# Second feed-forward matmul of a hybrid encoder block: groups 0 and 1 of the first pass interleaved, and a row load moved behind the pass

## The chip, the cores and the metric

The kernel runs on one core of one Trainium2 chip. The metric is the device time of one execution in microseconds (us), as the median of several runs. TensorE (PE) does the matmuls, VectorE (DVE) and ScalarE (ACT) prepare operands and evacuate results, GpSimd (POOL) does very little, and SyncE (SP) issues every DMA that loads weights, on one queue and in program order.

## The reference

One layer of an encoder block on 512 positions with 1024 channels, all in float32. What matters here is its end, the feed-forward part and the final norm:

```
xn = modulate(rmsnorm(h, norm2_g[l]), sh2, sc2)
ff = jnp.square(jax.nn.relu(xn @ w_ff1[l])) @ w_ff2[l]
h = h + g2[:, None, :] * ff
...
return rmsnorm(h, final_g)
```

`w_ff1` is 1024 x 4096 and `w_ff2` is 4096 x 1024. Before it come the two branches of the block (a gated MLP and a matrix-memory recurrence), which the change does not touch.

## The kernel before, in words

**Precision.** Every float32 matmul is made of three matmuls (`mm3`, L116 to L119): each operand is split into a high part (a copy rounded to the matmul's type, made on ScalarE) and a low part (the rest, a subtraction on VectorE), and the products high-high, low-high and high-low are added in PSUM. So for each operand there is one ACT instruction and one DVE instruction, and then TensorE can go on.

**The second feed-forward matmul.** The first 3072 of the 4096 rows of `w_ff2` are taken in six groups of 512 rows, `GROUPS = "WWSWWS"` (L1032). A "W" group is multiplied by Winograd's form of Strassen's scheme, with 7 products of half blocks in place of 8; an "S" group is multiplied plainly. The work is done in two passes over the six groups, because the PSUM banks hold only some of the sums at a time. In the first pass a W group has four products, P1, P2, P7 and P3, and in the second pass three (`later`, L1037). One product of one group is a **step**: two row halves of 128 positions times two k-tiles times three matmuls, so 12 matmuls of 128 x 512. The list `plan_` (L1131) says which sum each step adds to, and the loop at L1196 walks it; step 0 is its first entry. The banks of P1, P2, P7 and P3 (`gP1..`, `gP2..` and so on) are shared by all groups of the pass.

**The operands of a step.** The generator `passes` (L1096) yields them in the plan's order: a left operand out of the activations (`hl`, L1084: `hsh` on ACT at L1092 and `hsl` on DVE at L1093, 128 x 512) and a weight operand (`w_pair`, L1068: `wh` on ACT at L1075 and `wl` on DVE at L1076, 128 x 1024). The loop keeps five operand pairs made ahead (`prefetch_step(5)`). The names are numbered by step: `wh_g0`, `wh_g1`, `wh_g2`, `wh_x3`, `wh_x4`, `wh_g5` are steps 0 to 5; three of every five steps use the slots that the earlier matmul used too (`_g`, three buffers) and two use slots of their own (`_x`, two buffers, in a memory pool that opens with this stage).

**Where the weights come from.** For a W group the block of `w_ff2` has a left half (columns 0 to 511) in two pieces, `F11` and `F21`, and a right half in two pieces, `F12` and `F22`. Each piece is one DMA of 512 KB. P1 uses F11 and P2 uses F21 just as loaded. P7 needs the difference F22 - F12 (a DVE subtraction, L1106 in this version), and P3 uses F22. Left pieces are loaded into three buffers that the first feed-forward matmul also uses, so the first three are issued while that matmul still runs, and every split of a left piece frees its buffer for the next (`left.more()`). Right pieces go into a pool of four buffers that takes the place of the memory that held the first matmul's operands; it opens only when that matmul has read them (`x2s.close()`, `mhs.close()`, L1143 and L1144), and then four right pieces are asked for (L1150, L1151).

**The final norm's row.** `fing`, the vector `final_g` repeated over the 128 partitions (512 KB), is asked for at L1147, between the closing of the old pools and the first right pieces. Only the very last part of the kernel reads it (L1268).

**What sets the order.** The kernel is written in program order, and a scheduler then places each engine's instructions; each engine runs its own list strictly in that order. On SP the list is the order in which DMAs are issued: an entry that waits holds all entries behind it.

After the passes the last 1024 rows of `w_ff2` follow plainly (L1242), and then the gated residual and the final norm (L1253 on).

Of the kernel before, what the change touches and what calls it, by code (L numbers as in the profile page):

```python
# [16 lines left out]
P = 128  # L17
# [32 lines left out]
def block_kernel(ctx, tc, vecs_d, rows_d, ws_d, x_d, w_ada, w_in, w_out, w_ff1, w_ff2, out_d):  # L50
    nc = tc.nc
    act, dve, pool, pe, sp = nc.scalar, nc.vector, nc.gpsimd, nc.tensor, nc.sync
# [554 lines left out]
    n = 0  # L607
# [302 lines left out]
    hq = {}  # L910
# [121 lines left out]
    GROUPS = "WWSWWS"  # L1032
# [4 lines left out]
    def later(kind, pas):  # L1037
        return {("W", 0): ("P1", "P2", "P7", "P3"), ("W", 1): ("P5", "P6", "P4"),
                ("S", 0): ("P2", "P3", "P2", "P3"), ("S", 1): ("P4", "E", "P4", "E")}[kind, pas]
# [28 lines left out]
    def w_pair(src, feed=None):  # L1068
        i = count[0]
        count[0] += 1  # L1070
        if i % 5 < 3:
            wh, wl = wtile("wh", f"wh_g{i}", 2, 512), wtile("wl", f"wl_g{i}", 2, 512)
        else:
            wh, wl = (pass_pool[0].tile([P, 2, 512], F32R, tag="wx" + q, name=f"w{q}_x{i}", bufs=2) for q in "hl")
        act.copy(out=wh, in_=src)  # L1075
        dve.tensor_sub(out=wl, in0=src, in1=wh.bitcast(F32))  # L1076
        if feed:
            feed.more()
        return wh, wl
# [4 lines left out]
    def hl(src):  # L1084
        i = count[1]
        count[1] += 1
        if i < 2:
            both = fp.tile([P, 2, 2, 256], F32R, tag="sc", name=f"hs0{i}", bufs=2)
            h_, l_ = both[:, 0], both[:, 1]
        else:  # L1090
            h_, l_ = hs_tile("h"), hs_tile("l")
        act.copy(out=h_, in_=src)  # L1092
        dve.tensor_sub(out=l_, in0=src, in1=h_.bitcast(F32))  # L1093
        return h_, l_

    def passes():  # L1096
        for pas in range(2):
            for n, kind in enumerate(GROUPS):
                a11, a12, a21, a22 = hq[n, 0, 0], hq[n, 1, 0], hq[n, 0, 1], hq[n, 1, 1]
                if kind == "W" and pas == 0:  # L1100
                    yield hl(a11), w_pair(left.get(), left)
                    yield hl(a12), w_pair(left.get(), left)
                    b12, b22 = right.get(), right.get()
                    s3 = fp.tile([P, 2, 256], F32, tag="tmp", name=f"S3{n}", bufs=2)
                    dve.tensor_sub(out=s3, in0=a11, in1=a21)
                    dve.tensor_sub(out=b12, in0=b22, in1=b12)  # L1106
                    yield hl(s3), w_pair(b12, right)
                    dve.tensor_add(out=a21, in0=a21, in1=a22)
                    dve.tensor_sub(out=a11, in0=a21, in1=a11)
                    dve.tensor_sub(out=a12, in0=a12, in1=a11)  # L1110
                    yield hl(a12), w_pair(b22, right)
                elif kind == "W":
                    b11, b12 = left.get(), right.get()
                    dve.tensor_sub(out=b12, in0=b12, in1=b11)
                    left.more()
                    yield hl(a21), w_pair(b12)
                    b22 = right.get()
                    dve.tensor_sub(out=b22, in0=b22, in1=b12)
                    right.more()
                    yield hl(a11), w_pair(b22)  # L1120
                    b21 = left.get()
                    dve.tensor_sub(out=b21, in0=b21, in1=b22)
                    right.more()
                    yield hl(a22), w_pair(b21, left)
                else:
                    for a_ in ((a11, a12), (a21, a22))[pas]:
                        x_ = hl(a_)
                        yield x_, w_pair(left.get(), left)
                        yield x_, w_pair(right.get(), right)

    plan_ = [(pas, key) for pas in range(2) for kind in GROUPS for key in later(kind, pas)]  # L1131
    gen = passes()
    ready = []

# [9 lines left out]
    mhs.close()  # L1144
    hsp = ff.enter_context(tc.tile_pool(name="hsp", bufs=1, side="right"))
    fing = hsp.tile([P, D], F32, name="fing")
    sp.dma_start(out=fing, in_=rows_d[5].partition_broadcast(P))  # L1147
    ps_stack = ExitStack()
    pass_pool.append(ps_stack.enter_context(tc.tile_pool(name="passes", bufs=1, side="right")))
    for _ in range(4):  # L1150
# [45 lines left out]
    for i, (pas, key) in enumerate(plan_):  # L1196
        prefetch_step(5)
        (h_, l_), (wh, wl) = ready.pop(0)
        first = (key, 0) not in acc_b
        for t in range(2):  # L1200
            if first:
                acc_b[key, t] = bank(f"g{key}{t}")
            ts_ = slice(t * P, (t + 1) * P)
            for j in range(2):
                mm3(acc_b[key, t], h_[:, j, ts_], l_[:, j, ts_], wh[:, j], wl[:, j], first and j == 0,
                    i == last_of[key] and j == 1 and key not in ("P4", "E"))
        for key_ in jobs.get(i, ()):
            after(key_)
        if i == end0 + 6:
            for t in range(2):  # L1210
                gated("1", t, t, 0)
        if NS - i <= 4:
            ws_ff.prefetch(max(0, 4 - (NS - i)))
        if i == NS - 2:
            hs_pair(KF // 2)
# [111 lines left out]
```

## Time and profile before

| | |
|---|---|
| median of 3 runs | 813.99 us (813.52 to 814.81) |
| the profiled execution's own time | 815.62 us |
| span from its first to its last instruction | 813.8 us |
| mean granted TensorE clock over the span | 0.994 |
| TensorE matmul busy | 795.4 us (98% of the span) |
| VectorE busy | 615.3 us (76%) |
| ScalarE busy | 404.1 us (50%) |
| first matmul of the second feed-forward matmul | at 636.16 us of the span |

A row of the timeline has start, duration, engine, source line, operation, output and inputs, a count of merged instructions, and in brackets how long the engine had been idle before it and what ended that. Durations of neighbouring matmuls, and of neighbouring DVE or ACT instructions, overlap by a little, so the distance between starts is what a further instruction costs when nothing waits. A view of windows gives for each stretch its length, then for each engine the busy time and the number of instructions, then the granted clock of TensorE (1.00 is full speed), the share of time that the DMA engines were busy, and GB/s.

### The profile page before, as it was taken

What the parts mean: (1) busy time and instruction counts of PE and PEld (TensorE: products, weight loads), DVE (VectorE), ACT (ScalarE), POOL (GpSimd) and SP (SyncE); (2) the same over time, 40 slices, a digit from 0 to 9 for tenths busy, and PEclk for the clock granted to TensorE, in tenths of its full rate; (3) what the DMA queues carried; (4) which work ended last, traced back from release to release, by engine and by line L of the source; (5) the groups of instructions that cost most, each with busy time, mean ns of one, the idle gap of its engine ahead of it and who ended that gap; (6) DMA issues with size and microseconds to landing.
All of it is one profiled execution on the core that took longest, in us unless ns stands there. A gap on an engine that the chain in (4) does not pass through costs nothing.

```text
span 813.8 us, 11472 instructions
## 1 busy us (share of the span) xinstructions
PE 795.4 (98%) x4375; PEld 689.1 (85%) x4375; DVE 615.3 (76%) x925; ACT 404.1 (50%) x606; POOL 43.0 (5%) x62
## 2 busy tenths in 40 slices
PE   7999999999999999999999999999999799999996
PEld 6787888888988888888888899999999688888885
DVE  5889667684834367988756689988888898998936
ACT  5457556274432333242443446666666665555414
POOL 2004020121100000100000100000000000000000
PEclk9999999999999999999999999999999999999999
DMA  8974331143233398577345241333331676774302
GB/s 271 264 224 126 114 101 45 27 135 99 79 103 82 108 352 283 154 254 272 126 137 200 78 131 52 104 105 104 105 104 52 221 244 203 236 224 138 125 6 103
DMA packets 76423, 119.87 MB, mean 147 GB/s; under 512 B 5712, under 2 KB 38608, under 8 KB 76368
## 3 DMA queue, kind: packets, MB, share of 16 engines
q1 hardware_dynamic: 76368, 119.14, 46.0%
q8 instruction: 34, 0.56, 0.3%
q14 instruction: 21, 0.17, 0.1%
HBM read 117.02 MB, written 2.10 MB: 146 GB/s over the span
## 4 chain that ended last, share of the span: by engine, by line
PE 93%; DMA 2%; SPq 1%; ACT 1%; issue 1%; DVE 1%; POOLq 0%; POOL 0%
PE P L119 6%; PE P L117 6%; PE P L118 6%; PE gP L117 5%; PE gP L118 5%; PE gP L119 5%; PE qk L282 4%; PE wo L117 2%; PE wo L119 2%; PE wo L118 2%; PE f10b L118 1%; PE f10b L117 1%; PE f10b L119 1%; PE k1b L117 1%; PE o0b L119 1%
## 5 line engine op out<-in xcount | busy, mean ns | idle before, releaser
L1092 ACT CAST hsh<-h 128x512 fp32r<-128x512 f32 x38 | 23.6, 621 | 35.3 <-PE gP L118 27.2
L117 PE MATMUL gP<-wh_g,hsh 128*128 128x512 f32 x92 | 36.2, 396 | 0.2 <-ACT wh_g L1075 0.2
L118 PE MATMUL gP<-wl_g,hsh 128*128 128x512 f32 x92 | 35.8, 389 | 0.0
L119 PE MATMUL gP<-wh_g,hsl 128*128 128x512 f32 x92 | 35.8, 389 | 0.0
L1075 ACT CAST wh_g<-F 128x1024 fp32r<-128x1024 f32 x27 | 28.2, 1049 | 13.7 <-issue 7.1
L1076 DVE TENSOR_TENSOR wl_g<-F,wh_g 128x1024 fp32r<-128x1024 f32 x27 | 32.9, 1222 | 2.6 <-ACT wh_g L1075 2.5
L921 ACT CAST wh_T<-T 128x1024 fp32r<-128x1024 f32 x21 | 22.0, 1048 | 20.8 <-PE P L118 19.1
L118 PE MATMUL P<-x2l,wh_B 128*128 128x256 f32 x112 | 31.6, 282 | 0.0
L117 PE MATMUL P<-x2h,wh_B 128*128 128x256 f32 x112 | 31.6, 282 | 0.0
L119 PE MATMUL P<-x2h,wl_B 128*128 128x256 f32 x112 | 31.6, 282 | 0.0
L921 ACT CAST wh_B<-B 128x1024 fp32r<-128x1024 f32 x21 | 22.0, 1048 | 16.4 <-PE P L118 15.4
L1093 DVE TENSOR_TENSOR hsl<-h,hsh 128x512 fp32r<-128x512 f32 x38 | 25.9, 688 | 4.6 <-ACT hsh L1092 4.6
L117 PE MATMUL gP<-wh_x,hsh 128*128 128x512 f32 x60 | 23.8, 400 | 4.8 <-ACT wh_x L1075 4.8
L922 DVE TENSOR_TENSOR wl_T<-T,wh_T 128x1024 fp32r<-128x1024 f32 x21 | 25.7, 1224 | 2.6 <-ACT wh_T L921 2.5
L922 DVE TENSOR_TENSOR wl_B<-B,wh_B 128x1024 fp32r<-128x1024 f32 x21 | 25.6, 1220 | 0.0
L96 DVE TENSOR_TENSOR wl_gb<-raw_gb,wh_gb 128x1024 fp32r<-128x1024 f32 x8 | 9.8, 1224 | 19.7 <-ACT wh_gb L95 19.6
L118 PE MATMUL gP<-wl_x,hsh 128*128 128x512 f32 x60 | 23.7, 396 | 0.0
L119 PE MATMUL gP<-wh_x,hsl 128*128 128x512 f32 x60 | 23.6, 393 | 0.0
L667 DVE SCALAR_TENSOR_TENSOR accg<-arg,c_act,accg 128x1024 f32<-128x1024 f32 x14 | 18.0, 1283 | 5.6 <-DMA arg<-in_w_ada 5.5
L95 ACT CAST wh_ga<-raw_ga 128x1024 fp32r<-128x1024 f32 x8 | 8.4, 1051 | 27.2 <-PE ga0b L119 16.3
L1076 DVE TENSOR_TENSOR wl_x<-F,wh_x 128x1024 fp32r<-128x1024 f32 x17 | 20.7, 1222 | 1.4 <-ACT wh_x L1075 1.4
L118 PEld LDWEIGHTS P<-x2l,wh_B 128*128 128x128 f32 x112 | 21.3, 191 | 0.0
(610 smaller groups left out, 2815.5 us busy)
## 6 DMA issues: line engine op xcount, KB each, us to landing
F<-in_w_ff SPq DMA_DIRECT2D x48, 512.0 KB, 4.2
B<-in_w_ff SPq DMA_DIRECT2D x28, 512.0 KB, 3.8
ar<-in_w_ada SPq DMA_DIRECT2D x64, 128.0 KB, 3.4
arg<-in_w_ada SPq DMA_DIRECT2D x16, 512.0 KB, 5.9
raw_f<-in_w_ff SPq DMA_DIRECT2D x12, 512.0 KB, 3.3
raw_o<-in_w_in SPq DMA_DIRECT2D x8, 512.0 KB, 4.2
raw_mv<-in_w_in SPq DMA_DIRECT2D x8, 512.0 KB, 3.6
raw_gb<-in_w_in SPq DMA_DIRECT2D x8, 512.0 KB, 3.6
```

The lines of the kernel that those rows point to most:

```text
L96: dve.tensor_sub(out=wl, in0=raw, in1=wh.bitcast(F32))
L117: pe.matmul(out, lhsT=ah, rhs=bh, start=start, stop=False)
L118: pe.matmul(out, lhsT=ah, rhs=bl, start=False, stop=False)
L119: pe.matmul(out, lhsT=al, rhs=bh, start=False, stop=stop)
L282: pe.matmul(bk, lhsT=wx[:, kk, f * P:(f + 1) * P], rhs=xx[k], start=k == 0 and ps_ == 0, stop=k == KT - 1 and ps_ == 2)
L667: dve.scalar_tensor_tensor(out=acc, in0=raw, scalar=c_act[:, k:k + 1], in1=acc, op0=ALU.mult, op1=ALU.add)
L921: act.copy(out=wh, in_=src)
L922: dve.tensor_sub(out=wl, in0=src, in1=wh.bitcast(F32))
L1075: act.copy(out=wh, in_=src)
L1076: dve.tensor_sub(out=wl, in0=src, in1=wh.bitcast(F32))
L1092: act.copy(out=h_, in_=src)
L1093: dve.tensor_sub(out=l_, in0=src, in1=h_.bitcast(F32))
```

## The change

Two edits. First, in the first pass the four products that use left pieces only, P1 and P2 of group 0 and P1 and P2 of group 1, are yielded first and stand first in the plan; the products that need right pieces, P7 and P3 of group 0 and P7 and P3 of group 1, follow. From group 2 on nothing is altered, nor is the second pass. The number of instructions of each kind stays what it was. Second, the load of `fing` is no longer asked for ahead of the right pieces but in the loop, at the first pass's last step.

```diff
     def passes():
+        for n in range(2):
+            for nh in range(2):
+                yield hl(hq[n, nh, 0]), w_pair(left.get(), left)
         for pas in range(2):
             for n, kind in enumerate(GROUPS):
                 a11, a12, a21, a22 = hq[n, 0, 0], hq[n, 1, 0], hq[n, 0, 1], hq[n, 1, 1]
                 if kind == "W" and pas == 0:
-                    yield hl(a11), w_pair(left.get(), left)
-                    yield hl(a12), w_pair(left.get(), left)
+                    if n > 1:
+                        yield hl(a11), w_pair(left.get(), left)
+                        yield hl(a12), w_pair(left.get(), left)
                     b12, b22 = right.get(), right.get()
...
-    plan_ = [(pas, key) for pas in range(2) for kind in GROUPS for key in later(kind, pas)]
+    plan_ = [(0, key) for key in ("P1", "P2") * 2 + ("P7", "P3") * 2]
+    plan_ += [(0, key) for kind in GROUPS[2:] for key in later(kind, 0)]
+    plan_ += [(1, key) for kind in GROUPS for key in later(kind, 1)]
...
     fing = hsp.tile([P, D], F32, name="fing")
-    sp.dma_start(out=fing, in_=rows_d[5].partition_broadcast(P))
...
             after(key_)
+        if i == end0:
+            sp.dma_start(out=fing, in_=rows_d[5].partition_broadcast(P))
```

Since the names go by step, the same name means different work in the two versions: `wh_g2` is the difference for P7 of group 0 before, and piece F11 of group 1 now; `wh_x4` is F11 of group 1 before, and that difference now.

**The DMA queue of SP at the start of the stage**, before. In the names of the pieces the digit after F11, F21, F12 or F22 is the group; `fing` is the row of the final norm.

```order
L1053 DMA F11121_6235<-in_w_ff2 128x2x512
L1053 DMA F21120_6244<-in_w_ff2 128x2x512
L1053 DMA F12023_6265<-in_w_ff2 128x2x512
L1053 DMA F11219_6253<-in_w_ff2 128x2x512
L1147 DMA fing_6260<-in_rows 128x1024
L1053 DMA F22022_6267<-in_w_ff2 128x2x512
L1053 DMA F12121_6269<-in_w_ff2 128x2x512
L1053 DMA F22120_6271<-in_w_ff2 128x2x512
L1053 DMA F12219_6284<-in_w_ff2 128x2x512
```

The same place on SP now:

```order
L1053 DMA F11121_6235<-in_w_ff2 128x2x512
L1053 DMA F21120_6244<-in_w_ff2 128x2x512
L1053 DMA F12023_6264<-in_w_ff2 128x2x512
L1053 DMA F11219_6253<-in_w_ff2 128x2x512
L1053 DMA F22022_6266<-in_w_ff2 128x2x512
L1053 DMA F12121_6268<-in_w_ff2 128x2x512
L1053 DMA F22120_6270<-in_w_ff2 128x2x512
L1053 DMA F21218_6280<-in_w_ff2 128x2x512
L1053 DMA F11317_6290<-in_w_ff2 128x2x512
L1053 DMA F12219_6303<-in_w_ff2 128x2x512
L1053 DMA F22218_6330<-in_w_ff2 128x2x512
L1215 DMA fing_6260<-in_rows 128x1024
```

`fing` has moved from ahead of F22 of group 0 to behind the two right pieces of group 2; the scheduler placed it there, earlier than the last step of the pass at which the program asks for it.

**TensorE behind steps 0 and 1**, before. `gP10` is the bank of P1 for the first 128 positions, `gP11` for the second, and so on.

```order
L117 MATMUL gP10_6309<-wh_x4_6303,hsh5_6299 128x512
L117 MATMUL gP11_6316<-wh_x4_6303,hsh5_6299 128x512
L117 MATMUL gP70_6360<-wh_g2_6280,hsh3_6276 128x512
L117 MATMUL gP71_6367<-wh_g2_6280,hsh3_6276 128x512
L117 MATMUL gP30_6387<-wh_x3_6293,hsh4_6289 128x512
L118 MATMUL gP30_6387<-wl_x3_6294,hsh4_6289 128x512
L119 MATMUL gP30_6387<-wh_x3_6293,hsl4_6290 128x512
```

The same place on TensorE now, the start of step 2, and of it the rows that end step 3 and begin step 4:

```order
L117 MATMUL gP10_6305<-wh_g2_6276,hsh3_6272 128x512
L118 MATMUL gP10_6305<-wl_g2_6277,hsh3_6272 128x512
L119 MATMUL gP10_6305<-wh_g2_6276,hsl3_6273 128x512
...
L119 MATMUL gP21_6339<-wh_x3_6286,hsl4_6283 128x512
L117 MATMUL gP70_6406<-wh_x4_6299,hsh5_6295 128x512
L118 MATMUL gP70_6406<-wl_x4_6300,hsh5_6295 128x512
```

The scheduler had pulled two matmuls each of steps 4 and 2 ahead of step 3; now all 24 matmuls of P1 and P2 of group 1 come first, and P7 (step 4) follows.

**VectorE from the last evacuation of the first matmul on**, before. `hsl` and `wl` are low parts, S33 and the plain `h` rows are sums of activations, and a row that writes an F piece is the difference of two right pieces.

```order
L1029 TENSOR_TENSOR h710_6016<-h710_6016,P37_6203 128x512
L1093 TENSOR_TENSOR hsl3_6277<-S30_6273,hsh3_6276 128x512
L1093 TENSOR_TENSOR hsl4_6290<-h010_4529,hsh4_6289 128x512
L1105 TENSOR_TENSOR S33_6525<-h300_5070,h301_5071 128x512
L1093 TENSOR_TENSOR hsl5_6300<-h100_4596,hsh5_6299 128x512
L1108 TENSOR_TENSOR h301_5071<-h301_5071,h311_5073 128x512
L1093 TENSOR_TENSOR hsl6_6324<-h110_4598,hsh6_6323 128x512
L1093 TENSOR_TENSOR hsl7_6351<-S31_6347,hsh7_6350 128x512
L1109 TENSOR_TENSOR h100_4596<-h101_4597,h100_4596 128x512
L1105 TENSOR_TENSOR S34_6619<-h400_5307,h401_5308 128x512
L1110 TENSOR_TENSOR h110_4598<-h110_4598,h100_4596 128x512
L1106 TENSOR_TENSOR F12023_6265<-F22022_6267,F12023_6265 128x1024
```

The same place on VectorE now (L1110 is now the difference of right pieces, L1113 the sum of activations):

```order
L1029 TENSOR_TENSOR h710_6016<-h710_6016,P37_6203 128x512
L1076 TENSOR_TENSOR wl_g2_6277<-F11121_6235,wh_g2_6276 128x1024
L1093 TENSOR_TENSOR hsl3_6273<-h100_4596,hsh3_6272 128x512
L1113 TENSOR_TENSOR h100_4596<-h101_4597,h100_4596 128x512
L1093 TENSOR_TENSOR hsl4_6283<-h110_4598,hsh4_6282 128x512
L1076 TENSOR_TENSOR wl_x3_6287<-F21120_6244,wh_x3_6286 128x1024
L1110 TENSOR_TENSOR F12023_6264<-F22022_6266,F12023_6264 128x1024
L1093 TENSOR_TENSOR hsl5_6296<-S30_6292,hsh5_6295 128x512
L1093 TENSOR_TENSOR hsl6_6323<-h010_4529,hsh6_6322 128x512
L1076 TENSOR_TENSOR wl_g5_6327<-F22022_6266,wh_g5_6326 128x1024
L1076 TENSOR_TENSOR wl_x4_6300<-F12023_6264,wh_x4_6299 128x1024
L1110 TENSOR_TENSOR F12121_6268<-F22120_6270,F12121_6268 128x1024
```

Two splits of left pieces now stand ahead of the first row that needs a right piece; before, that row came ahead of every split of step 2 and later.

## The prediction

> **What bounds the kernel now.** I read the page first: who is busy, and at what clock.
>
> ```profile
> span 813.8 us, 11472 instructions
> PE 795.4 (98%) x4375; PEld 689.1 (85%) x4375; DVE 615.3 (76%) x925; ACT 404.1 (50%) x606; POOL 43.0 (5%) x62
> PE   7999999999999999999999999999999799999996
> ```
>
> TensorE is the bound: 18.4 us of the span are not matmul, and in the row of slices only three are below 9: the start, the end, and one slice between 630 and 651 us, where the second feed-forward matmul begins. The other engines have room on average. So the question is what TensorE waits for in that one slice. I asked the view of waits for TensorE alone, from 630 us to the end:
>
> ```profile
> PE gP L117 <- ACT wh_x L1075: 4.8, 1, 4.8
> PE gP L117 <- ACT wh_g L1075: 0.2, 1, 0.2
> ```
>
> Two waits, at one place, and none in the 160 us after it. The timeline of TensorE shows the place: the stage's first matmul, the last of step 1, the wait, and the first matmul of step 5.
>
> ```profile
> 636.16 0.40 PE L117 MATMUL gP<-wh_g,hs 128*128 128x512 f32 x1
> ...
> 641.40 0.39 PE L119 MATMUL gP<-wh_g,hs 128*128 128x512 f32 x1
> 646.55 0.77 PE L117 MATMUL gP<-wh_x,hsh 128*128 128x512 f32 x2 [4.76 <-ACT wh_x L1075]
> 647.50 1.22 PE L117 MATMUL gP<-wh_g,hsh 128*128 128x512 f32 x2 [0.17 <-ACT wh_g L1075]
> ...
> 650.83 0.39 PE L118 MATMUL gP<-wl_g,hsh 128*128 128x512 f32 x1
> ...
> 656.73 0.39 PE L117 MATMUL gP<-wh_g,hsh 128*128 128x512 f32 x1
> ...
> 663.53 0.39 PE L117 MATMUL gP<-wh_g,hsh 128*128 128x512 f32 x1
> ```
>
> From 656.73 to 663.53 there are 30 matmuls, so one costs 0.227 us and a step of 12 costs 2.72. After the wait the first matmuls stand wider apart than that. The windows show why, by the granted clock (the number before the DMA share):
>
> ```profile
> 19.00:22.50 3.50, 2.47 (x14) 1.84 (x14) 2.58 (x12) 2.62 (x6) 0.00 (x0) 1.00 0.99 282
> 22.50:25.90 3.40, 3.40 (x10) 2.66 (x9) 3.38 (x9) 2.13 (x4) 0.00 (x0) 0.50 0.82 252
> ...
> 647.10:650.50 3.40, 3.23 (x8) 2.42 (x8) 3.40 (x4) 1.81 (x3) 0.00 (x0) 0.50 0.65 185
> ```
>
> For 3.4 us after the wait the clock was 0.50. Who was the wait for? ScalarE's cast and VectorE's subtraction both waited for a DMA:
>
> ```profile
> 644.51 1.99 ACT L1075 CAST wh_x<-F 128x1024 fp32r<-128x1024 f32 x2 [4.39 <-DMA F<-in_w_ff]
> ```
>
> ```profile
> 644.58 1.22 DVE L1106 TENSOR_TENSOR F<-F,F 128x1024 f32<-128x1024 f32 x1 [1.45 <-DMA F<-in_w_ff]
> ```
>
> That is piece F22 of group 0. The cast of step 4 (piece F11 of group 1, loaded long before) stood behind it on ScalarE, and TensorE waited for that cast.
>
> **What the wait costs as a whole.** By its parts: after the matmul at 641.40 the next was due at 641.63 and came at 646.55, 4.92 us. From 646.55 to 650.83 there are 10 matmuls, worth 2.27 us; they took 4.28, so 2.01 are lost to the clock and the wait of 0.17. Together 6.93. As a check, step 5 was due five steps after 636.16, at 636.16 + 60 x 0.227 = 649.78, and began at 656.73: 6.95 late. I use 6.95.
>
> **Edit 1, the order of the steps.** It adds no instruction. TensorE is to go through steps 2 and 3 (P1 and P2 of group 1, left pieces alone) while the right pieces land, so P7 comes at 636.16 + 48 x 0.227 = 647.05 instead of before it can be fed. What hides the wait is then these 24 matmuls, 5.44 us; without that cover the wait is back. I check each operand by walking ScalarE's and VectorE's lists with these rows:
>
> ```profile
> 636.36 0.62 ACT L1092 CAST hsh<-S 128x512 fp32r<-128x512 f32 x1 [0.72 <-PE P L119]
> ...
> 637.41 0.63 ACT L976 ACTIVATE h<-h 128x512 f32<-128x512 f32 x1
> ```
>
> ```profile
> L1076 DVE TENSOR_TENSOR wl_g<-F,wh_g 128x1024 fp32r<-128x1024 f32 x11 | 13.4, 1222 | 1.4 <-ACT wh_g L1075 1.4
> L1093 DVE TENSOR_TENSOR hsl<-h,hsh 128x512 fp32r<-128x512 f32 x14 | 9.5, 688 | 2.4 <-ACT hsh L1092 2.4
> L1106 DVE TENSOR_TENSOR F<-F,F 128x1024 f32<-128x1024 f32 x4 | 4.9, 1222 | 2.2 <-DMA F<-in_w_ff 2.2
> ```
>
> ```profile
> L1075 ACT CAST wh_g<-F 128x1024 fp32r<-128x1024 f32 x12 | 12.5, 1048 | 6.2 <-DVE F L1106 2.7 <-PE gP L119 2.1 <-issue 1.4
> ```
>
> Step 2: its piece F11 of group 1 has long landed; its buffer for the high part comes free with the first matmul's last product, at 636.36 (the same releaser as the cast quoted above). The cast ends at 637.4, the low part at 638.6, `hsl` at 639.4. Needed at 641.63: two microseconds to spare. Step 3: on ScalarE two casts of 0.62 and two activations of 0.63 stand ahead of `wh_x3`, so it ends by 641.0 and its low part by 642.2, needed at 644.35. Its piece F21 of group 1 was issued at 633.36 and took 3.7, so it is there at 637.1.
>
> ```profile
> 633.36 2.74 SPq L1053 DMA_DIRECT2D F<-in_w_ff  x3
> ```
>
> ```profile
> DMA to landing us min/median/max: 3.7/3.7/3.7
> ```
>
> Step 4, P7 of group 0, is the tight one. On VectorE there stand, from the landing of F22 of group 0 on: the difference (1.22), `hsl5`, `hsl6` (0.69 each), `wl_g5` and `wl_x4` (1.22 each), 5.04 in full durations, about 4.7 by the distances between starts. TensorE's second matmul of step 4 reads `wl_x4` at 647.05 + 0.23 = 647.28. So F22 has to land by about 642.4. When does it?
>
> **Edit 2, `fing` out of the queue.** Issues and landings around it before; these are the issue of the piece ahead of `fing`, `fing`, and then F22 of group 0, F12 and F22 of group 1:
>
> ```profile
> 635.74 0.37 SPq L1053 DMA_DIRECT2D F<-in_w_ff  x1
> ```
>
> ```profile
> DMA to landing us min/median/max: 4.8/4.8/4.8
> ```
>
> ```profile
> 636.36 0.84 SPq L1147 DMA_DIRECT2D fing<-in_rows  x1
> 637.25 1.45 SPq L1053 DMA_DIRECT2D F<-in_w_ff  x3
> ```
>
> ```profile
> fing<-in_rows SPq DMA_DIRECT2D x1, 512.0 KB, 6.8
> ```
>
> ```profile
> L1053 SPq DMA_DIRECT2D F<-in_w_ff x3: 428/469/469, 637.2 to 638.2; - x3
> ...
> DMA to landing us min/median/max: 7.2/8.1/8.9
> ```
>
> The piece ahead landed at 635.74 + 4.8 = 640.5, `fing` at 643.2, F22 of group 0 at 637.25 + 7.2 = 644.45. The three right pieces were issued half a microsecond apart (637.25, 637.7, 638.2) and landed at 644.45, 645.8 and 647.1, 1.3 apart: the queue was full, a piece costs it 1.3, and `fing` cost 2.6. Without `fing` ahead, F22 is issued at about 636.2, as soon as SP is free of the entry of 635.74, and lands at 640.5 + 1.35 = 641.85. That is my value; the bounds are 639.5 (issue plus 3.3, just under the 3.7 that an undisturbed piece took) and 645.1 (issue plus the slowest, 8.9). At 641.85 `wl_x4` is ready between 646.55 and 646.9, or 647.2 if VectorE is still at `wl_x3` until 642.17: 0.1 to 0.7 before it is needed. So TensorE doesn't wait, but narrowly. Step 5 needs `wl_g5`, which comes earlier. Steps 6 and 7 need the difference of group 1 (F22 landed by 644.5) and then 0.69 + 0.69 + 1.22 + 1.22: ready at about 651.2 to 652.3 against 652.7 for step 6, and 1.3 us in hand for step 7. In the plain group behind them VectorE has one `hsl` per two steps, and catches up.
>
> Where `fing` goes costs nothing: on SP the pieces behind it are those of group 3, whose P7 is step 14, due at 636.16 + 168 x 0.227 = 674.3; a delay of 2.6 in a load asked for near 651 is far from that, and `fing` itself is read only in the final norm, behind every step. Behind the stage nothing else moves, and TensorE has no other wait, so the whole 6.95 comes off the end: the profiled execution from 815.62 to 808.67, the median, 1.63 lower, from 813.99 to **807.0**.
>
> **The rivals.** Those who want to see a change of this kernel need about 0.2%, 1.6 us; 812.4 and 815.6 are the borders.
>
> *P7's operand is late.* If F22 of group 0 still lands at 644.45 (the queue holds it for another reason than `fing`), `wl_x4` is ready at 649.2 to 649.5 and TensorE waits 2.0 at step 4: 809.0. For it: the slack is a few tenths. Against it: landings in a full queue follow each other at 1.3. The clock is a second price. [...] The trace agrees for the wait of 4.76, with a clock of 0.50 for 3.4 us behind it; but the slice from 19.00 to 22.50, with 1.03 idle in 3.50 and no long gap, is also followed by 0.50 from 22.50 to 25.90. By that row a wait of 2.0 can bring another 2.0 with it: 811.0.
>
> *VectorE becomes the bound.* Its busy time from 636 to 710 has to fit into 7 us less:
>
> ```profile
> 636.00:641.60 5.60, 5.24 (x9) 1.00 0.87 313
> ...
> 670.00:690.00 20.00, 15.96 (x18) 1.00 0.59 191
> 690.00:710.00 20.00, 19.92 (x24) 1.00 0.77 241
> sum 74.00, DVE 66.09; mean DVE 11.02
> ```
>
> 66.1 of 67.05 would be 99%. If 1 to 2 us of it find no room, 808 to 809. Against: from 670 to 690 it was idle a fifth of the time, because its five operand pairs ahead were made; it reaches that state again in the first plain group.
>
> *The wait only moves.* If F22 lands between about 646 and 649, step 4 waits 3.5 to 6.5 and the clock takes 2.0: within 1.6 of before, about 813.5. That needs an issue to landing of 10 us or more, where 8.9 was the longest.
>
> *Slower.* VectorE runs in strict order, and the difference for P7 now stands ahead of `hsl5`, `hsl6` and both splits of steps 4 and 5. One mechanism makes it slower: F22 lands after 649.1. Then step 4 waits T + 4.75 - 647.28, 6.6 or more, and 2.0 of clock follow: over 6.95 + 1.6. At a landing of 650 that is 7.5 + 2.0 - 6.95 = 2.5 lost, 816.5. It decides from a landing 12.9 us after the issue; nothing in the trace took that long.
>
> **How the numbers follow.** My forecast 0.78 (807.0); P7 late 0.10 (809.0 to 811.0); VectorE the bound 0.06 (808 to 809); the wait only moves 0.03 (813.5); slower 0.03 (816.5). The low end is the forecast less the 0.5 by which the fastest run of before lay under its median and 0.3 for the gain: 806.2. The high end takes in VectorE as the bound and the late operand without the clock, 809.0, and the 0.8 by which the slowest run of before lay over the median: 809.8. The first three cases are faster: 0.94; same 0.03; slower 0.03.
>
> **What would show it.** Right: no wait of TensorE over 0.3 us between 636 and 663, the clock at 1.00 there, step 5's first matmul near 649.8, F22 of group 0 landing near 641.9, and every later row of TensorE 6.9 earlier. Wrong: a wait at the first or second matmul of step 4 with VectorE's `wl_x` or ScalarE's `wh_x` as its releaser (late operand), waits spread over steps 12 to 19 (VectorE), or a stage as short as this with the time given back behind 710.

## The result, and the profile after

| | before | now |
|---|---|---|
| median of 5 runs each, taken alternately | 814.81 us (813.52 to 816.16) | 808.74 us (806.53 to 811.59) |
| ratio, with its 95% interval | | 0.9929 (0.9899 to 0.9958) |
| the profiled execution's own time | 815.62 us | 807.55 us |
| its span | 813.8 us | 805.7 us |
| first matmul of the stage | 636.16 us | 634.99 us |
| from there to the end of TensorE | 170.33 us | 163.42 us |

The change makes the kernel faster by 0.7%, 6.07 us by the two medians. "Stage" below is always the stretch of the last row, from the first matmul into a `gP` bank to the end of the last matmul. It is the number by which the traces are compared, since two traces of the same kernel can begin the stage over 2 us apart (636.16 and 633.91, both of the kernel before).

The page of the changed kernel first: span, TensorE's and the other engines' busy time, then TensorE's row of slices.

```profile
span 805.7 us, 11465 instructions
PE 794.0 (99%) x4375; PEld 688.8 (85%) x4375; DVE 613.6 (76%) x925; ACT 404.9 (50%) x606; POOL 43.0 (5%) x62
PE   8999999999999999999999999999999999999996
```

The slice with a 7 between 630 and 651 us is a 9 now. The view of waits for TensorE, from 20 to 806 us, has two entries, and both lie before the stage:

```profile
PE qk L282 <- ACT xs L369: 0.3, 1, 0.3
PE k1b L117 <- ACT wh_k L95: 0.2, 1, 0.2
```

The timeline of TensorE shows the same place as in the prediction: the first matmul, the first of step 2, the first two of step 4 (P7 of group 0), the first of step 5, and the last matmul of the kernel.

```profile
634.99 0.40 PE L117 MATMUL gP<-wh_g,hs 128*128 128x512 f32 x1
...
640.45 0.39 PE L117 MATMUL gP<-wh_g,hsh 128*128 128x512 f32 x1
...
645.89 0.39 PE L117 MATMUL gP<-wh_x,hsh 128*128 128x512 f32 x1
646.12 0.39 PE L118 MATMUL gP<-wl_x,hsh 128*128 128x512 f32 x1
...
648.65 0.39 PE L117 MATMUL gP<-wh_g,hsh 128*128 128x512 f32 x1
...
798.02 0.39 PE L119 MATMUL gE<-wh_f,hsl 128*128 128x512 f32 x1
```

Step 5 begins 13.66 us after the first matmul; before it began 20.57 after it (656.73 - 636.16). The last matmul before was this one:

```profile
806.10 0.39 PE L119 MATMUL gE<-wh_f,hsl 128*128 128x512 f32 x1
```

So the stage was 806.10 + 0.39 - 636.16 = 170.33 and is 798.02 + 0.39 - 634.99 = 163.42: 6.91 shorter, and all of it is gained by step 5. The other 1.17 of the 8.1 by which the spans differ lies ahead of the stage. The windows (columns as before) show the clock at 1.00 where it was 0.50, and VectorE over the first 74 us of the stage, the stretch in which the prediction looked at it:

```profile
647.10:650.50 3.40, 3.40 (x17) 2.80 (x16) 3.40 (x5) 3.25 (x6) 0.00 (x0) 1.00 0.88 287
634.99:708.85 73.86, 73.86 (x328) 61.08 (x327) 70.63 (x83) 46.49 (x60) 0.00 (x0) 1.00 0.74 251
```

How tight step 4 is, VectorE's timeline tells: the low part of step 3, the difference of right pieces, the low part `hsl5`, and the splits of steps 5 and 4.

```profile
639.22 1.22 DVE L1076 TENSOR_TENSOR wl_x<-F,wh_x 128x1024 fp32r<-128x1024 f32 x1
641.24 1.23 DVE L1110 TENSOR_TENSOR F<-F,F 128x1024 f32<-128x1024 f32 x1 [0.80 <-DMA F<-in_w_ff]
642.38 0.68 DVE L1093 TENSOR_TENSOR hsl<-S,hsh 128x512 fp32r<-128x512 f32 x1
...
643.58 1.22 DVE L1076 TENSOR_TENSOR wl_g<-F,wh_g 128x1024 fp32r<-128x1024 f32 x1
644.72 1.22 DVE L1076 TENSOR_TENSOR wl_x<-F,wh_x 128x1024 fp32r<-128x1024 f32 x1
```

`wl_x4` ends at 644.72 + 1.22 = 645.94 and is read at 646.12: 0.18 to spare. The DMA for which VectorE waited until 641.24 is F22 of group 0. Its own view of issue and landing, and ahead of it that of the piece in front:

```profile
L1053 SPq DMA_DIRECT2D F<-in_w_ff x1: 368/368/368, 634.6 to 634.6; - x1
DMA to landing us min/median/max: 5.0/5.0/5.0
...
L1053 SPq DMA_DIRECT2D F<-in_w_ff x1: 463/463/463, 635.0 to 635.0; - x1
DMA to landing us min/median/max: 6.2/6.2/6.2
```

The piece ahead landed at 639.6 and F22 at 641.2, 1.6 behind it and 6.2 after the first matmul; before it was 8.3 after it (644.45 - 636.16). `fing` was issued at 646.4 and took 5.9, so it landed at 652.3; TensorE waits for nothing behind it.

### The profile page after: what moved, and what is told of

Same layout as the page of the kernel before. It is cut to its first block, busy times and chain, and to the rows that moved or that the text cites. A ratio compares the mean times of both kernels' runs of the same rounds, so it can differ in the third digit from the quotient of the medians.

```text
span 805.7 us, 11465 instructions
## 1 busy us (share of the span) xinstructions
PE 794.0 (99%) x4375; PEld 688.8 (85%) x4375; DVE 613.6 (76%) x925; ACT 404.9 (50%) x606; POOL 43.0 (5%) x62
## 4 chain that ended last, share of the span: by engine, by line
PE 95%; DMA 1%; SPq 1%; DVE 1%; issue 1%; ACT 1%; POOLq 0%; POOL 0%
PE P L117 6%; PE P L118 6%; PE P L119 6%; PE gP L117 5%; PE gP L118 5%; PE gP L119 5%; PE qk L282 4%; PE wo L117 2%; PE wo L119 2%; PE wo L118 2%; PE f10b L118 1%; PE f10b L117 1%; PE f10b L119 1%; PE k1b L117 1%; PE o0b L119 1%; PE gb0b L118 1%
## 5 line engine op out<-in xcount | busy, mean ns | idle before, releaser
L119 PEld LDWEIGHTS P<-x2h,wl_B 128*128 128x128 f32 x112 | 21.3, 190 | 0.0
L117 PEld LDWEIGHTS P<-x2h,wh_B 128*128 128x128 f32 x112 | 21.3, 190 | 0.0
```

The source lines that it names most:

```text
L117: pe.matmul(out, lhsT=ah, rhs=bh, start=start, stop=False)
L119: pe.matmul(out, lhsT=al, rhs=bh, start=False, stop=stop)
```

## The experiments

Twelve runs follow; five of them are kernels run again unaltered. Times of a kernel are set beside runs of the kernel before on the same chip; "F22" in what follows is F22 of group 0, and its landing is given as the time after the stage's first matmul at which the first reader started on it.

### The two edits apart

`e1_order_only` is the changed kernel with the row back at its old place:

```diff
+    sp.dma_start(out=fing, in_=rows_d[5].partition_broadcast(P))
...
-        if i == end0:
-            sp.dma_start(out=fing, in_=rows_d[5].partition_broadcast(P))
```

> The new order of the steps alone; the row load stays ahead of the right pieces. My theory (the row costs the queue 2.6 us, and the 24 matmuls of steps 2 and 3 cover 5.44 us): F22 of group 0 lands 8.3 us after the stage's first matmul, as before the change; VectorE has here the difference, wl_g5, one sum and wl_x4 behind it (about 4.1 us by the distances between starts), so the low part of step 4 is ready 12.5 us after the stage's first matmul and is needed at 11.1: TensorE waits 1.0 to 2.0 us at step 4. Time 5 to 6 us under the kernel before if the clock stays at 1.00 behind so short a wait, 3 to 4 under it if the clock goes to 0.50 for 3.4 us. Rival (where the row stands makes no difference, the landing is set by when the pool opens): no wait, and the time of the changed kernel, 7 under before.

`e2_row_only` is the kernel before with the same lines moved the other way.

> The row load moved behind the right pieces, the order of the steps as before. My theory: F22 of group 0 lands 1.8 to 2.6 us earlier and the wait of TensorE in front of step 4's first matmul shrinks from 4.76 to 2.2 to 3.0 us. [...] Rival (where the row stands makes no difference): a wait of 4.8 us and the time of before.

Measured: `e1_order_only` 809.0 us (807.62 to 811.02), ratio 0.9929 (0.9914 to 0.9944), stage 164.69; `e2_row_only` 812.13 us (811.88 to 812.91), ratio 0.9964 (0.9952 to 0.9976), stage 168.66. The timeline of TensorE in `e1_order_only` has one wait, at the second matmul of step 4:

```profile
645.56 0.63 PE L117 MATMUL gP<-wh_x,hsh 128*128 128x512 f32 x2
647.19 0.51 PE L118 MATMUL gP<-wl_x,hsh 128*128 128x512 f32 x1 [1.00 <-DVE wl_x L1076]
```

That in `e2_row_only` has the wait of before, shorter:

```profile
642.57 0.74 PE L117 MATMUL gP<-wh_x,hsh 128*128 128x512 f32 x2 [2.84 <-ACT wh_x L1075]
643.52 0.73 PE L117 MATMUL gP<-wh_g,hsh 128*128 128x512 f32 x2 [0.21 <-ACT wh_g L1075]
```

And its windows show that the clock was still lost behind it:

```profile
640.94:644.36 3.42, 1.58 (x6) 1.01 (x7) 3.42 (x4) 3.42 (x4) 0.00 (x0) 1.00 0.64 222
644.36:647.77 3.41, 3.41 (x10) 2.65 (x9) 3.41 (x4) 0.24 (x2) 0.00 (x0) 0.50 0.88 284
```

So edit 1 carries the gain: alone it takes 5.64 off the stage of before, edit 2 alone 1.67, both 6.91. These are single traces, and the stage of before alone differs by 0.9 between three of them (below); by the runs' medians the two are worth 5.87 and 2.74 (809.0 and 812.13 against 814.87). The stage's gains don't add up (7.31), because both work on one wait: edit 2 alone brings F22 2 us earlier (6.4 in place of 8.4) and the wait from 4.76 to 2.84, with the half clock still to pay; behind edit 1, F22 at 8.4 costs 1.00 and no clock, and edit 2 takes that last wait away. Behind the first edit the second one's share is small: 809.0 against the changed kernel's 808.74 of the first runs tells nothing apart, but against its second set on the same chip (`e4_after_again` below, 806.96) it is 2.0, and the intervals of the two ratios (0.9914 to 0.9944, and 0.9884 to 0.9913) don't overlap.

### P3 ahead of P7, and the changed kernel again

`e3_p3_first` takes P3 of groups 0 and 1 ahead of P7, so that step 4 needs no difference (the plan alone is shown; the generator yields in the same order):

```diff
...
-    plan_ = [(0, key) for key in ("P1", "P2") * 2 + ("P7", "P3") * 2]
+    plan_ = [(0, key) for key in ("P1", "P2") * 2 + ("P3", "P7") * 2]
```

> The changed kernel, but in groups 0 and 1 P3, which needs F22 as loaded, comes before P7, which needs the difference: step 4 is fed by a cast and a split instead of by a difference, two hsl and two splits. My theory: TensorE has no wait in the stage, and step 4's low part is ready 1 us or more before it is needed instead of 0.2. The time is that of the changed kernel, since it does not wait there either; within 1 us of it. Rival (the narrow slack of step 4 sometimes fails and makes the spread of the changed kernel's runs, 806.5 to 811.6): the runs lie closer together, within 2.5 us, and the median is 1 to 2 us under the changed kernel's.

`e4_after_again` is the changed kernel, unaltered.

> The changed kernel once more, for its spread and for comparison on the same chip. My theory: 6 to 8 us under the kernel before, no wait of TensorE over 0.3 us in the stage, clock 1.00 there. The runs differ by 2 to 5 us, from waits in the first 30 us and their half-clock stretches, which the change doesn't touch. Rival (slack at step 4 fails in some executions): this profile shows a wait of 0.3 us or more at step 4.

Measured: 807.74 us (807.11 to 808.65), ratio 0.9911 (0.9898 to 0.9923), and 806.96 us (806.65 to 808.29), ratio 0.9899 (0.9884 to 0.9913). Neither trace has a wait of TensorE in the stage, and both stages are 163.39. More slack at step 4 buys nothing, so the 0.18 was enough in the traces taken. F22 was there at 6.0 in both.

### Half the cover

`e5_half_cover` puts one step of left pieces, 12 matmuls, in front of P7 and not two (again the plan alone):

```diff
...
-    plan_ = [(0, key) for key in ("P1", "P2") * 2 + ("P7", "P3") * 2]
+    plan_ = [(0, key) for key in ("P1", "P2", "P1", "P7", "P3", "P2", "P7", "P3")]
```

> The changed kernel, but only P1 of group 1 goes ahead of P7 of group 0; P2 of group 1 follows after P3 of group 0. The cover is 12 matmuls, 2.72 us, instead of 24. My theory: F22 lands 6.0 to 6.5 us after the stage's first matmul, P7 is due at 8.2 and its first matmul needs the difference (1.2) and a cast (1.05): TensorE waits 0.3 to 1.0 us there and up to 1 us more for the low part, 1 to 2 us in all. The clock stays at 1.00, since in the runs so far a wait of 1.0 left it so and one of 2.8 halved it; time 5 to 6 us under the kernel before. Rival (one product is cover enough): no wait and the time of the changed kernel.

Measured: 808.83 us (807.85 to 812.79), ratio 0.9928 (0.9907 to 0.9949), stage 164.36. TensorE's timeline has two small waits:

```profile
643.49 0.73 PE L117 MATMUL gP<-wh_x,hsh 128*128 128x512 f32 x2 [0.18 <-ACT wh_x L1075]
644.43 0.73 PE L117 MATMUL gP<-wh_x,hsh 128*128 128x512 f32 x2 [0.21 <-ACT wh_x L1075]
```

Half the cover loses about 1 us of the 6.9. The scheduler had a part in this: behind the first two matmuls of P7 it set two each of the next two steps, as it had done in the kernel before.

### A later F22

`e6_row_twice` is `e1_order_only` with most of the row loaded once more behind it (960 of 1024 columns, into a tile that nothing reads):

```diff
+    fing2 = hsp.tile([P, 960], F32, name="fing2")
+    sp.dma_start(out=fing2, in_=rows_d[5][0:960].partition_broadcast(P))
```

> The new order of the steps, with the row load ahead of the right pieces and a second load of 960 of its columns, into a tile that nothing reads, behind it. My theory (F22 lands later by what stands ahead of it in a full queue, and the wait of TensorE grows by as much): F22 lands 9.6 to 10.4 us after the stage's first matmul instead of 8.3, and TensorE waits 2.2 to 3.5 us at step 4 instead of 1.0. By the row of the run with a wait of 2.8, the clock is then halved for 3.4 us: in all 4 to 5.5 us lost, time 1.5 to 3 us under the kernel before. [...]

`e7_f22_twice` is `e1_order_only` with F22 loaded a second time into the same tile, which can't be read before the second load has landed:

```diff
                 sp.dma_start(out=raw, in_=w_ff2[r0:r0 + 256, jh * 512:(jh + 1) * 512].rearrange("(k p) c -> p k c", p=P))
+                if nm == "F22" and n == 0 and len(self.todo) > 12:
+                    sp.dma_start(out=raw, in_=w_ff2[r0:r0 + 256, jh * 512:(jh + 1) * 512].rearrange("(k p) c -> p k c", p=P))
```

> The new order of the steps, the row load ahead of the right pieces, and piece F22 of group 0 loaded twice into the same place, so that P7 and P3 of group 0 must wait for the second landing. My theory: the second load is issued when the first has landed, 8.5 us after the stage's first matmul, and lands at 12 to 13. P7 is due at 10.9 and its first matmul needs 2.3 us behind the landing: a wait of 3.5 to 5 us, and the clock halved: 6 to 7 us lost, about the time of the kernel before (within 1.5 us). The advantage of the new order is then gone. Rival of the prediction (a late F22 makes the new order slower than the old): over 1.6 us slower than the kernel before.

Measured: `e6_row_twice` 810.01 us (808.23 to 813.04), ratio 0.994 (0.992 to 0.9961), stage 167.58; `e7_f22_twice` 814.76 us (812.68 to 816.55), ratio 0.9992 (0.9978 to 1.0007), stage 170.78. The waits of TensorE in the two timelines:

```profile
647.44 1.22 PE L117 MATMUL gP<-wh_x,hsh 128*128 128x512 f32 x2 [2.33 <-ACT wh_x L1075]
```

```profile
649.91 1.22 PE L117 MATMUL gP<-wh_x,hsh 128*128 128x512 f32 x2 [4.14 <-ACT wh_x L1077]
```

In `e7_f22_twice` ScalarE's cast of F22 started 12.2 after the first matmul (634.70):

```profile
646.92 1.99 ACT L1077 CAST wh_g<-F 128x1024 fp32r<-128x1024 f32 x2 [0.67 <-DMA F<-in_w_ff]
```

So the new order gives back what it gained when F22 lands 12.2 after the first matmul, and it isn't slower than before even there.

`e6_row_twice` has the wait and the half clock that were expected, but not the time: 1.5 to 3 us under the kernel before was expected, and the medians are 5.2 apart (815.2 and 810.01). The one trace was a late draw: in two more traces of the same kernel, below, F22 came earlier and the clock stayed.

### The clock

`e8_filled_wait` is the kernel before with 20 matmuls behind step 1 whose stationary operand is zero, so that they add nothing to the sums (`zero_r` is made of zeros at the kernel's start):

```diff
...
+        if i == 1:
+            for r in range(20):
+                pe.matmul(acc_b["P1", r % 2], lhsT=zero_r, rhs=wh[:, r % 2], start=False, stop=False)
```

> The kernel before, with 20 matmuls of a stationary operand of zeros, which add nothing to the sums of P1, put behind step 1: TensorE works through most of its wait. The steps behind them stand in a slightly other order (two matmuls of step 4 no longer come first), so the first useful matmul comes about 0.9 us later than before. My theory (idle time halves the clock): the clock stays at 1.00, the 2.0 us of the half clock are saved and 0.9 are lost, so time 0.5 to 1.5 us under the kernel before. Rival (the half clock comes from something else in this stretch, such as the full DMA queue): 0.50 for 3.4 us as before, and 0.5 to 1 us slower.

Measured: 813.63 us (812.11 to 816.66), ratio 0.9989 (0.9976 to 1.0002), stage 170.61, and the clock at 1.00 throughout the stage. The timeline of TensorE, the fill and the wait that was left:

```profile
640.27 4.83 PE L1211 MATMUL gP<-wh_g,zero_r 128*128 128x512 f32 x20
647.17 0.73 PE L119 MATMUL gP<-wh_g,hsh 128*128 128x512 f32 x2 [2.07 <-ACT wh_g L1077]
```

In this stage the half clock is a consequence of TensorE's idleness: with most of the idle time filled, and 2.07 of it left, it did not come in this trace. The stage gained nothing against the trace of before all the same, since F22 was there at 9.4 in this run and at 8.4 before, and a matmul of another step waited first; beside `e9_before_again` below, with F22 at 9.0, it is 0.54 shorter. The experiment shows the cause and not the price.

Looked at together, the ten traces then showed more than a length. In the trace of before the clock of 0.50 began at 22.47 and 647.11. They are 624.64 apart, 183 times 3.4133, and the other stretches at 0.50 lie on such a grid too, which lies elsewhere in each trace: the last of before began at 810.95, 48 steps behind 647.11, and the two of the changed kernel's trace, from 14.85 and 803.32, are 231 steps apart. One step of the grid is called a cell below. To see whether position is by the grid or at a fixed distance behind the wait, the kernel before was taken twice more (`e9_before_again`, `e10_before_third`), and `e6_row_twice` twice more (`e11_row_twice_again`, `e12_row_twice_third`), all unaltered, one trace each.

> The kernel before, unchanged, for one more trace. In the ten traces so far every stretch at the granted clock of 0.50 begins on a grid of 3.4133 us that runs through the whole trace (before: 22.47 and 647.11, 183 steps apart), and the grid lies elsewhere in each trace. Theory (grid): what counts is how much TensorE idles within one cell of the grid. In the stage a cell with 1.84 to 3.1 us idle was followed by a cell at 0.50, cells with 1.0 to 1.55 were not, and one with 1.91 was not. So the wait of about 4.8 is always followed by at least one cell at 0.50, beginning at a grid point 0 to 3.4 us behind the moment at which the cell with most of the wait ends, and the stage is 170.0 to 170.6 with one and up to 172.3 with two. The stage starts at 634.0 to 634.2 if no cell of the first 26 us is at 0.50, 634.6 to 635.0 with one near 14, and 635.7 to 636.3 with one near 22.5 or two. Rival (length): a half-clock stretch follows the wait at a fixed distance, as in the trace of before, 0.56 behind the first matmul after it, whatever the grid; then the stage is 170.3 again.

> The kernel before, unchanged, once more. As for the run ahead of it: the grid theory has the half-clock stretch begin at a point that lies a whole number of 3.4133 us from the other half-clock stretches of the same trace, another distance behind the wait than in the other traces of before; the rival has it 0.56 behind the first matmul after the wait.

> The kernel with edit 1 and the row asked for twice ahead of the right pieces, unchanged, for one more trace. Its wait was 2.33 and lay in one cell of the grid (644.01 to 647.42, 2.31 idle), and a cell at 0.50 followed: stage 167.58. Grid: if the wait falls into one cell again by more than 1.9, the same. If a grid point cuts it so that no cell holds more than 1.5 (chance about a third), no cell at 0.50 follows, and the stage is about 165.8 (163.4 and the wait). Rival (length): a wait of 2.3 always brings 3.41 us at 0.50, stage 167.6.

> The same kernel once more, for another position of the grid. Grid: stage about 167.6 if one cell holds over 1.9 of the wait, about 165.8 if none holds over 1.5; between them open. Rival (length): 167.6 whatever the grid.

| | time, us | stage | F22 at | wait | stretch at 0.50 in the stage |
|---|---|---|---|---|---|
| `e9_before_again` | 816.37 | 171.15 | 9.0 | 5.41 | 6.83 from 644.63 |
| `e10_before_third` | 813.24 | 170.22 | 7.9 | 4.28 | 6.83 from 641.69 |
| `e11_row_twice_again` | 809.82 | 164.95 | 9.8 | 1.27 | none |
| `e12_row_twice_third` | 809.29 | 164.38 | 9.2 | 0.66 | none |

The windows of `e9_before_again`, cut along its grid: its stretch at 0.50 near the start, the cell with most of the wait, and the stretch behind it.

```profile
13.16:19.98 6.82, 6.82 (x25) 5.95 (x26) 5.33 (x16) 3.67 (x7) 0.00 (x0) 0.50 0.90 259
641.22:644.63 3.41, 0.52 (x3) 0.09 (x1) 1.85 (x4) 0.00 (x0) 0.00 (x0) 1.00 1.02 366
644.63:651.46 6.83, 4.31 (x10) 3.19 (x11) 6.29 (x6) 4.41 (x5) 0.00 (x0) 0.50 0.56 177
```

From 13.16 to 644.63 are 185 steps of 3.4133. In its timeline the wait ends like this:

```profile
647.15 1.22 PE L117 MATMUL gP<-wh_x,hsh 128*128 128x512 f32 x2 [5.41 <-ACT wh_x L1075]
```

So the clock fell 2.5 us before TensorE resumed, where in the trace of before it fell 0.56 after that. In `e10_before_third` the wait ended at 643.81, and the windows show that the clock fell 2.1 before:

```profile
638.27:641.69 3.42, 1.26 (x6) 0.72 (x4) 2.60 (x5) 0.00 (x0) 0.00 (x0) 1.00 0.99 355
641.69:648.51 6.82, 4.70 (x11) 3.52 (x12) 6.67 (x6) 4.41 (x5) 0.00 (x0) 0.50 0.62 197
```

So the fixed distance falls, and the grid stands. What a cell needs to bring the next one down is read from the windows of single cells. Of before:

```profile
640.29:643.70 3.41, 1.50 (x7) 0.92 (x5) 2.84 (x5) 0.00 (x0) 0.00 (x0) 1.00 0.92 343
643.70:647.11 3.41, 0.56 (x2) 0.30 (x2) 2.53 (x3) 2.60 (x3) 0.00 (x0) 1.00 0.46 175
```

Of `e6_row_twice`, and then of `e8_filled_wait`:

```profile
644.01:647.42 3.41, 1.11 (x5) 0.57 (x4) 2.52 (x3) 2.54 (x4) 0.00 (x0) 1.00 1.01 381
647.42:650.83 3.41, 3.39 (x8) 2.71 (x9) 3.41 (x5) 2.11 (x3) 0.00 (x0) 0.50 0.76 250
```

```profile
643.24:646.65 3.41, 1.86 (x8) 1.15 (x7) 2.40 (x3) 2.47 (x3) 0.00 (x0) 1.00 0.40 152
646.65:650.06 3.41, 2.89 (x12) 2.19 (x13) 3.41 (x4) 1.94 (x3) 0.00 (x0) 1.00 0.54 182
```

TensorE's busy time taken from the length gives the idle time of a cell. Cells of this stage at full speed with 1.55 (`e8_filled_wait`) and less were followed by full speed; those with 2.16 (`e10_before_third`) and more by 0.50. In between the rows disagree: 1.91 in before was followed by full speed, 1.84 in `e2_row_only` by 0.50. So in these traces the border lies between 1.55 and 2.16 of 3.41 idle, and idle time alone does not draw it sharply. It is a border for these matmuls. Near the kernel's start, where others run, idle time is not the measure: in before the slice from 19.00 to 22.50 with 1.03 idle was followed by 0.50, and the cell from 8.82 with 1.50 idle by full speed. In the changed kernel's trace a cell without any idle time was followed by 0.50:

```profile
11.44:14.85 3.41, 3.41 (x32) 3.37 (x31) 2.86 (x9) 1.38 (x3) 0.00 (x0) 1.00 0.97 255
14.85:18.26 3.41, 3.41 (x10) 2.63 (x9) 3.41 (x10) 2.44 (x5) 0.00 (x0) 0.50 0.94 271
```

What brings the clock down there stays open.

The waits of `e11_row_twice_again` and `e12_row_twice_third` came out too short (1.27 and 0.66 where 2.33 was expected), so that a grid point cutting a wait of 2.3 in two was not seen. What the two runs do show is that F22's landing itself moves by up to 1.7 us between runs of one kernel (10.8, 9.8, 9.2), and that TensorE's loss follows it. Most of that is the row. In the three traces of before it took 6.8, 7.3 and 6.2 from issue to landing, and F22 landed about 1.4 behind it in each; with the row twice the second load of it took 8.0, 7.7 and 7.0. In the five traces with no row ahead of F22, F22 was there at 6.0 to 6.4. So the second edit takes a load that varies out of F22's way, and not only 2 us.

The grid was also expected to explain when the stage starts. In two of the four traces it did (`e9_before_again` 636.11 and `e11_row_twice_again` 635.82, each with two cells at 0.50 near the start); `e10_before_third` at 633.91 and `e12_row_twice_third` at 635.85 did not fit. What sets the start of the stage, 633.9 to 636.2 over all traces, stays open.

## Why the prediction was right, and where its steps were off

**The sum.** The wait and its clock were put at 6.95; the stage is 6.91 shorter in the changed kernel's trace and 6.94 in `e4_after_again`. Against the two later traces of before it is 7.73 and 6.80 shorter; in those F22 was there at 9.0 and 7.9, and the clock was lost for two cells. The 6.95 was right for the trace from which it was worked out, and is one draw of a quantity that varies by about 1 us.

**The cover.** Named were the 24 matmuls of P1 and P2 of group 1, 5.44 us. In the trace they run from 640.45 to 645.89, 5.44, and no wait is left. Half of them (`e5_half_cover`) loses 1.0. That edit 1 alone would leave a wait at the second matmul of step 4 for `wl_x` was the first rival's picture, and `e1_order_only` shows it.

**The landing of F22.** This term was mis-sized. Taken was 5.69 after the first matmul (641.85 - 636.16); it was 6.2, and 6.0 in `e4_after_again`. The piece ahead landed 4.6 after the first matmul and not 4.34, and F22 1.6 behind it and not 1.35. VectorE had an idle 0.80 just before it, so the later landing went straight into the slack, which came out at 0.18, within the 0.1 to 0.7 given. "TensorE doesn't wait, but narrowly" held.

**The place of `fing`.** It cost nothing, as expected: issued at 646.4, landed at 652.3, and no wait of TensorE until the end.

**The late operand.** The rival priced a landing at 8.3 at a wait of 2.0. `e1_order_only` has that landing and waits 1.00. The step that failed is the list of VectorE: it was walked as it stands in the changed kernel, with the difference ahead of the `hsl`s, but the scheduler writes another list when the row is ahead of F22. The timeline of VectorE in `e1_order_only`:

```profile
640.02 0.68 DVE L1093 TENSOR_TENSOR hsl<-S,hsh 128x512 fp32r<-128x512 f32 x1
640.62 0.68 DVE L1093 TENSOR_TENSOR hsl<-h,hsh 128x512 fp32r<-128x512 f32 x1
641.22 0.68 DVE L1093 TENSOR_TENSOR hsl<-S,hsh 128x512 fp32r<-128x512 f32 x1
643.04 1.23 DVE L1110 TENSOR_TENSOR F<-F,F 128x1024 f32<-128x1024 f32 x1 [1.14 <-DMA F<-in_w_ff]
```

Three `hsl` are done before the piece lands, and two of them are in the 4.75 that the prediction counted from the landing on. One sum of activations stands there in their place, so `wl_x4` was ready 4.2 behind the landing. The rest of the difference is on TensorE: its list has a second matmul ahead of the one that reads `wl_x4` (the x2 in its row at 645.56), and a wait is counted from the end of the matmul before it. The stage lost 1.27 in all. For the changed kernel itself, with F22 late by chance, the price of the prediction still stands untested: its list has the difference first.

**The clock's two prices.** The prediction left open whether a wait of 2.0 costs the clock (809.0 without, 811.0 with). A wait of 2.33 did in `e6_row_twice` and one of 2.84 in `e2_row_only`; 2.07 didn't in `e8_filled_wait`, where a grid point cut it into 1.55 and 0.52. So the length of the wait is the wrong measure: what counts in this stage is how much of one cell is idle (2.30 in `e6_row_twice`, 1.84 in `e2_row_only`). That a wait much shorter than the 4.76 of before can cost the clock, which the prediction allowed for, came out right by luck: the row from 19.00 that the prediction rested it on is from the kernel's start, where idle time is not the measure (above). The price was put at 2.0. Stage less 163.42 less the waits gives 1.98 for before, 2.19 for `e2_row_only` and 1.83 for `e6_row_twice`, but 3.14 for `e7_f22_twice`, where these cells follow each other:

```profile
645.45:648.87 3.42, 0.32 (x2) 0.00 (x0) 3.23 (x4) 2.56 (x4) 0.00 (x0) 1.00 0.91 332
648.87:652.28 3.41, 2.29 (x5) 1.38 (x6) 3.41 (x4) 2.89 (x4) 0.00 (x0) 0.50 0.47 158
652.28:655.69 3.41, 3.41 (x9) 2.64 (x10) 3.20 (x4) 0.00 (x0) 0.00 (x0) 0.50 0.76 256
```

A cell that is already at 0.50 and has 1.12 idle was followed by another one at 0.50.

**VectorE as the bound.** It did not become one. Over the first 73.86 us of the stage it was busy for 70.63, 96%, and TensorE waited for nothing there.

**Slower.** The crossing was put at a landing 12.9 after the first matmul (649.1 - 636.16). `e7_f22_twice`, at 12.2, is level with before (0.9992, interval 0.9978 to 1.0007). Its wait of 4.14 was shorter than the formula's 5.85 (12.22 + 4.75 - 11.12), though the operand came later than the formula has it. This is the split of step 4 on VectorE:

```profile
650.79 1.22 DVE L1078 TENSOR_TENSOR wl_x<-F,wh_x 128x1024 fp32r<-128x1024 f32 x1
```

It ends at 652.01, 5.1 behind the start of the cast of F22 and not 4.75. TensorE resumed ahead of it, at 649.91, because its list had matmuls that don't read `wl_x4` first. The clock loss was higher. Nothing was run beyond that.

**The time.** The median is 1.74 above the 807.0 and inside the range, while the profiled execution, 807.55, is 1.12 below the 808.67 forecast for it. The latter is the 1.17 by which the stage began earlier. The former is spread: of the first five runs two (810.42 and 811.59) lie above the whole range, and the four runs of `e4_after_again` lie between 806.65 and 808.29; over all nine the median is 807.55. The run of 811.59 has a mean granted clock of 0.991 on record where the profiled one has 0.996, so more of it ran at 0.50; the run of 810.42 has 0.995, which doesn't set it apart. Where the two lost their time has no trace and stays open.

## What to carry to other kernels

When a wait is seen, ask what is in hand at that moment that doesn't need the late data: here 24 matmuls, put in front by order alone, were worth two to three times as much as making the data 2 us earlier (5.87 and 2.74 by the runs' medians, 5.64 and 1.67 by one trace each). Price an operand's chain on the lists of the kernel that is to run, not on those of another version: a scheduler that knows of the late load writes other lists. And a bottleneck engine's wait can have a second price behind it in the clock (here 1.8 to 3.1 us behind waits of 2.33 to 5.41, none behind those of 0.66 to 2.07), which depends on where the wait falls, so one trace of a wait is one draw.

## What the runs showed of the hardware

- The stretches at a granted clock of 0.50 stood on a grid of 3.4133 us that ran through a whole execution and lay elsewhere in the next one (183 steps from 22.47 to 647.11 in before, 185 from 13.16 to 644.63 in `e9_before_again`, 184 from 13.63 to 641.69 in `e10_before_third`). In the second feed-forward matmul a cell of the grid at full speed with 2.16 us or more idle was followed by one at 0.50, one with 1.55 or less was not; of two between, 1.84 was and 1.91 was not. Near the kernel's start a cell without idle time was followed by 0.50 too.
- The fall came while the wait still lasted (2.5 us before TensorE resumed in `e9_before_again`, 2.1 in `e10_before_third`) and then hid in it in part: 6.83 at 0.50 cost 2.32 beyond the wait in `e9_before_again` (171.15 - 163.42 - 5.41), 3.41 cost 1.98 in before.
- With loads close behind one another in the queue, F22 and the two 512 KB pieces behind it landed 1.3 to 1.6 behind the load ahead of each, in before and in the changed kernel's trace. The row of the same size, one row written to all 128 partitions, landed 2.6 behind the piece ahead in that of before (643.2 and 640.5), and moving it away brought F22 forward by about 2 (8.4 to 6.4 in `e2_row_only`).
